# A third set of block products, its third weight block in half tiles, and stationary tiles at multiples of 128 bytes

## The chip, the cores and the metric

The kernel runs on one core of a Trainium2 chip. The metric is the time of one execution on the device in microseconds (us); smaller is better. A trace of one execution by the hardware profiler is read beside it. In the text PE is TensorE, DVE is VectorE, ACT is ScalarE, POOL is GpSimd, SP is SyncE, which issues most loads.

## The reference

The input `x` is 256 tokens by 2048. `h` is its RMS norm, and `h @ w_in` (2048 x 18,448) gives eleven groups of columns:

```
a_q a_k (1024 each)  a_v a_g (2048 each)  a_lr (16)      gated linear attention, 4 heads
b_q b_k b_v b_g (2048 each)                              differential attention, 16 heads
m_a m_b (2048 each)                                      merge gates
y_a = (rmsnorm(gla(a_q, a_k, a_v, a_lr)) * silu(a_g)) @ w_branch_a
y_b = (rmsnorm(diff(b_q, b_k, b_v)) * 0.8 * silu(b_g)) @ w_branch_b
out = x + rmsnorm((sigmoid(m_a) * y_a + sigmoid(m_b) * y_b) @ w_out)
```

All of it is float32.

## The kernel before

**A product in three.** A float32 operand is split into a high part (rounded to the type that TensorE takes at full speed, by ScalarE) and a low part (the rest, by VectorE). One product is three matmuls: high by high, low by high and high by low. `x` is split once, into `xs`. Every weight is loaded, split and used once: `emit_half` (line 215) takes a half tile of 128 x 1024 weights from the list `seq`, issues the load if it is the first half of a 1 MB tile, and has ScalarE write `hi` and VectorE write `lo`. `take` (line 239) hands a half to the matmuls and emits up to `AHEAD` = 4 halves past it. There are three `raw`, three `hi` and three `lo` buffers in `wpool`.

**Three ways to use a half.** `half_tile` (line 399), for token-major keys such as `v4`, `ag0`, `dv0`, `bg0`, `y00`, `o0`, does 12 matmuls of 512 columns with a slice of `xs` (or `oah`, `oal`, `obh`, `obl`, `mh`, `ml`) as the stationary tile and weights streaming. `half_channel` (line 420), for keys and queries, has the weights as stationary tile: 8 matmuls of 512 columns (line 427) and 8 of 256 (line 429). `block_products` (line 625) is the third.

**Sets.** A set is 1024 columns of `w_in`, done as a 2 x 2 block product with seven products in place of eight (Strassen's scheme). The operands of `x` are slices of `xs` (products 1, 2, 4) or sums of its blocks that `sum_operands` has split beforehand into eight tiles `s4h`, `s4l`, `r1h` and so on (products 3, 5, 6, 7). The order is 1, 3, 5, 6, 2, 7, 4. Each product has four steps (two tiles, two halves) of 6 matmuls of 512 columns (line 648). The weight operands are made in place, in four `chain` tiles of 1 MB: `a` starts as one block and `b` as another; after product 1 a DMA on POOL's queue that adds in flight (line 188) adds the second block to `a`; VectorE adds `b` to `a` before each step of product 6 (line 179); after product 6 the second block is added to `b` in the same way; the third block, `raw_c`, is product 2's operand, and VectorE adds it to `a` after each of that product's steps (line 186). `raw_c` is loaded as two 1 MB tiles, into two of the three `raw` slots (line 175). `link` (line 158) loads `a` and `b`. Two sets exist; their columns are the first and second half of one merge gate, and their results, `left` and `right`, become tanh values that are spilled to DRAM.

**Order of the work.** The first value groups of the linear attention come first (about 0 to 81 us). Then the mixed phase (81 to 277 us): `phase_steps` (line 70) spreads 40 other steps evenly between the 56 steps of the sets: 8 of `v4`, then 32 halves of the keys and queries of the linear attention. After it come the gates `ag0` to `ag3`, merge gates `m00` and `m01`, `diff_heads(0)` and `diff_heads(1)`, the branch product `y0`, `diff_heads(2)` and `diff_heads(3)`, the rest of the merge gates, `y1`, and `w_out`. `diff_heads(g)` (line 913) does values `dv` and gates `bg` of four heads by `token_major`, then eight query and key blocks by `channel_major`. Attention itself is cut into small tasks (generators): `pump(n)` (line 365) runs one step of the first `n` tasks in the list, between stretches of weight matmuls. `gla_scores` and `gla_out` are the linear attention's, `diff_split` and `diff_pair` the differential attention's. `y0` needs both `gla_out` tasks.

**Memory.** Pools lie one behind the other in the order in which they are opened: `const`, `wpool`, `big` (18 slots of 4 KB a partition, for `u` tiles), then `first`, which is closed after the mixed phase and followed by `small` and `more` (13 slots, for `u2` tiles). In the memory map of the compiled program `wpool` begins at byte 23,328 of a partition and `big` at 72,480, both 32 past a multiple of 128; `xs`, `mh`, `ml`, `hi` and `lo` therefore all lie 32 past one. The eight sum tiles in `first` begin at 193,888 and `more` at 165,472, both 96 past one; `oah`, `oal`, `obh`, `obl`, `ath` and `atl` lie in `more`.

Of the kernel before, what the change touches and what calls it, by code (L numbers as in the profile page):

```python
# [6 lines left out]
F32 = mybir.dt.float32  # L7
F32R = mybir.dt.float32r
# [17 lines left out]
ROWS = {"two": 2, "tok": 4, "chan": KT}  # L26
WARM = 8
PRODUCTS = (1, 3, 5, 6, 2, 7, 4)
BIG = 18
MORE = 13  # L30
BRIDGE = 512
# [3 lines left out]
def chunk_plan():  # L35

    plan = [("v0", "two", "w_in", [(6144, RANK), (2048, 2 * VG[0] - RANK)])]
    at = 2 * VG[0] - RANK
    for g, n in enumerate(VG[2:]):
        plan.append((f"v{g + 2}", "tok", "w_in", [(2048 + at, n)]))  # L40
        at += n
    for hf in range(2):
        for name, base in (("k", 1024), ("q", 0)):
            for c in range(4):
                plan.append((f"{name}{hf}{c}", "chan", "w_in", [(base + 512 * hf + P * c, P)]))
    o = 6144 + RANK
    for s in range(2):
        plan.append((f"set{s}", "set", "w_in", [(o + 10240 + 1024 * s, 1024)]))
    for g in range(4):
        plan.append((f"ag{g}", "tok", "w_in", [(4096 + 512 * g, 512)]))  # L50
        plan.append((f"dv{g}", "tok", "w_in", [(o + 4096 + 512 * g, 512)]))
        plan.append((f"bg{g}", "tok", "w_in", [(o + 6144 + 512 * g, 512)]))
        for c in range(4):
            for n, name in enumerate(("dq", "dk")):
                plan.append((f"{name}{g}{c}", "chan", "w_in", [(o + 2048 * n + 512 * g + P * c, P)]))
        plan.append((f"m0{g}", "tok", "w_in", [(o + 8192 + 512 * g, 512)]))
        for br in range(2):
            plan.append((f"y{br}{g}", "tok", ("w_branch_a", "w_branch_b")[br], [(512 * g, 512)]))
        plan.append((f"o{g}", "tok", "w_out", [(512 * g, 512)]))
    return plan  # L60
# [22 lines left out]
def hybrid_kernel(ctx: ExitStack, tc, xt, xn, preg, postg, w, w2, gkb, glag, lamv, diffg, ident_d, causal_d, lmask_d, out):  # L83
# [24 lines left out]

    def t2(shape, name):
        count[0] += 1  # L110
        return pools[0].tile(shape, F32, tag="t2", name=f"{name}_{count[0]}", bufs=6 if len(pools) == 1 else 8)

    def spill(t, name):
        count[0] += 1
# [25 lines left out]
    def halves_of(*keys):  # L140
        return [(key, r, h) for key in keys for r in range(len(at[key])) for h in range(2)]

    def heads_order(g):
        return halves_of(f"dv{g}", f"bg{g}", *(f"{name}{g}{c}" for pair in range(2) for name in ("dq", "dk") for c in (2 * pair, 2 * pair + 1)))
# [10 lines left out]
    def weights(key, r):  # L155
        a, size = at[key][r]
        return w[a : a + P * size].rearrange("(p n) -> p n", p=P), size

    def link(s, name, t):
        count[0] += 1  # L160
        c = pools[0].tile([P, 2048], F32, tag="chain", name=f"{name}_{count[0]}", bufs=4)
        sp.dma_start(c, weights(f"set{s}", {"a": 0, "b": 6}[name] + t)[0])
        chain[s, name, t] = c

    def emit_set(s, prod, t, h):
        c = slice(1024 * h, 1024 * h + 1024)
        if h == 0 and prod == 1:
            if s == 0:
                link(s, "a", t)
            link(s, "b", t)  # L170
        if h == 0 and prod == 4 and s == 0:
            link(1, "a", t)
        if h == 0 and prod == 2:
            count[0] += 1
            raws[s, t] = wpool.tile([P, 2048], F32, tag="raw", name=f"raw_c_{count[0]}")
            sp.dma_start(raws[s, t], weights(f"set{s}", 4 + t)[0])
# [3 lines left out]
        return (raws[s, t] if prod == 2 else b if prod in (3, 7) else a)[:, c]  # L180

    def follow_set(s, prod, t, h):
        c = slice(1024 * h, 1024 * h + 1024)
        a, b = chain[s, "a", t], chain[s, "b", t]
        if prod == 2:
            dve.tensor_tensor(out=a[:, c], in0=a[:, c], in1=raws[s, t][:, c], op=ALU.add)
        if h == 1 and prod in (1, 6):
            pool.dma_start(a if prod == 1 else b, weights(f"set{s}", 2 + t)[0], accum_op=ALU.add)

# [344 lines left out]
    def sum_operands():  # L534
# [5 lines left out]
        temps = []  # L540
        for n in range(2):
            count[0] += 1
            temps.append(pools[0].tile([P, 2, 8, P], F32, tag="chain", name=f"temp_{count[0]}", bufs=4))
        r1, s2, r3, s4 = (temps[n // 2][:, n % 2] for n in range(4))

        def part(i, j, q):
# [42 lines left out]
        pump()  # L589


    gspill = [None] * 4
    ts = {}

    def others():
# [29 lines left out]
    def block_products(s):  # L625
# [2 lines left out]
        left, right = u([P, 2, 512], "gl"), u([P, 2, 512], "gr")  # L628
        kept = {}

        def squash(dst, scale):
            act.activation(dst, dst, AF.Tanh, scale=scale)

        for prod in PRODUCTS:
            if prod not in bank:
# [2 lines left out]
            for t in range(2):  # L638
                for h in range(2):
# [10 lines left out]
                    if t and h:  # L650
                        if prod in (1, 5):
                            kept[prod] = t2([P, 512], f"p{prod}")
                            act.activation(kept[prod], out, AF.Copy)
                        if prod == 5:
                            kept[3] = t2([P, 512], "p35")
                            dve.tensor_tensor(out=kept[3], in0=bank[3], in1=kept[5], op=ALU.add)
                        if prod == 6:
                            dve.tensor_tensor(out=right[:, 0, :], in0=x, in1=kept[3], op=ALU.add)
                            squash(right[:, 0, :], minus_half[:, 0:1])
                        if prod == 2:  # L660
                            dve.tensor_tensor(out=left[:, 0, :], in0=out, in1=kept[1], op=ALU.add)
                            squash(left[:, 0, :], half_rstd[:, 0:1])
                        if prod == 7:
                            dve.tensor_tensor(out=right[:, 1, :], in0=x, in1=kept[5], op=ALU.add)
                            squash(right[:, 1, :], minus_half[:, 1:2])
                            gspill[2 * s + 1] = spill(right, "gr")
                        if prod == 4:
                            act.activation(left[:, 1, :], x, AF.Tanh, scale=half_rstd[:, 1:2])
                            gspill[2 * s] = spill(left, "gl")
                    yield  # L670

    sets = (step for s in range(2) for step in block_products(s))
    rest = others()
    for step in phase_steps():
        next(sets if step[0] == "set" else rest)
    for gen in (sets, rest):
        assert next(gen, DONE) is DONE
    joint.close()
    pools[0] = ctx.enter_context(tc.tile_pool(name="small", bufs=2))
    pools.append(ctx.enter_context(tc.tile_pool(name="more", bufs=MORE)))  # L680
    tasks.append(forget_gate())


# [227 lines left out]
        yield  # L911

    def diff_heads(g):
        banks = token_major(f"dv{g}", 512, x_ops, 2)
        late_u = u2 if g > 1 else u
        vv = late_u([P, 2, 512], "dv")
        for b in range(2):
            act.activation(vv[:, b, :], banks[b], AF.Copy, scale=rstd[:, b : b + 1])
        banks = token_major(f"bg{g}", 512, x_ops, 2)
        uu = late_u([P, 2, 512], "ub")  # L920
        for b in range(2):
            gate(banks[b], b, uu[:, b, :])
# [66 lines left out]
    def settle():  # L989
        while tasks:  # L990
            pump()
        gb.extend(fetch(d, "gateb", u) for d in gspill)

    mh = [u([P, 4, S], "mh", F32R) for _ in range(4)]
    ml = [u([P, 4, S], "ml", F32R) for _ in range(4)]
# [150 lines left out]
```

## Time and profile before

| | us |
|---|---|
| median of 3 runs (lowest, highest) | 1149.97 (1147.6, 1150.31) |
| the profiled execution's own time | 1149.55 |
| its span, first to last instruction | 1147.7 |
| PE busy | 1127.6 |
| DVE busy | 761.0 |
| ACT busy | 640.9 |
| POOL busy | 71.6 |

The mean granted TensorE clock of the core is 0.994 of full speed. The busy time of PE has the overlap of neighbouring matmuls in it, so it says that PE rarely stands still, and not how far it is from its best. Lines such as L407 are lines of the kernel before.

### The profile page before, as it was taken

To read this page: it belongs to the slowest core of one execution; us is meant where nothing else is said; L and a number is where in the kernel's file an instruction comes from. 1 tells how busy PE (TensorE), PEld (TensorE's weight loads), DVE (VectorE), ACT (ScalarE), POOL (GpSimd) and SP (SyncE) were. 2 spreads that over 40 slices of the span, in tenths; PEclk is the share of its full clock that TensorE was granted. 3 is DMA by queue.
4 is the path that set the end of the run, shared out by engine and by line. 5 is a ranking of instruction groups with operands and counts; after the bars stand their busy time and mean duration, and the time that the engine had idled before them with its cause. 6 is when DMAs were issued, how large, how long until landed. Compare 5 with 4: busy or idle time off the path is not lost.

```text
span 1147.7 us, 14888 instructions
## 1 busy us (share of the span) xinstructions
PE 1127.6 (98%) x5642; PEld 961.2 (84%) x5642; DVE 761.0 (66%) x1088; ACT 640.9 (56%) x957; POOL 71.6 (6%) x101
## 2 busy tenths in 40 slices
PE   9999999999999999999999999999999999999996
PEld 7999788788888888888888888888888888888886
DVE  7878876777579974577567555447666765565462
ACT  7856565556756554575656444446665665444460
POOL 0110000102031010100000000000000100000000
PEclk9999999989999999999999999999999999999998
DMA  8798777755555566355455544555455565555751
GB/s 312 263 358 226 225 294 215 193 184 184 183 190 178 200 238 257 118 177 182 148 202 186 197 164 172 182 197 176 175 173 182 191 226 177 174 179 209 275 196 74
DMA packets 37783, 230.48 MB, mean 201 GB/s; under 512 B 4752, under 2 KB 6288, under 8 KB 14672
## 3 DMA queue, kind: packets, MB, share of 16 engines
q1 hardware_dynamic: 31392, 204.89, 50.6%
q0 software_dynamic: 5312, 23.33, 7.5%
q10 hardware_dynamic: 1008, 1.32, 0.3%
q8 instruction: 44, 0.72, 0.3%
q14 instruction: 27, 0.22, 0.1%
HBM read 220.08 MB, written 9.44 MB: 200 GB/s over the span
## 4 chain that ended last, share of the span: by engine, by line
PE 93%; DMA 3%; ACT 1%; DVE 1%; issue 1%; DVEq 0%; SPq 0%; POOLq 0%; POOL 0%; ACTq 0%
PE mm L407 55%; PE mm L427 10%; PE mm L648 5%; PE mm L429 5%; PE bg L427 4%; PE bg L429 2%; DMA raw_c<-in_w_dram 2%; PE bg L390 2%; PE mm L375 2%; PE mm L390 2%; PE bg L407 1%; PE bg L748 1%; DMA raw<-in_w_dram 1%; PE bg L375 1%; PE bg L859 1%
## 5 line engine op out<-in xcount | busy, mean ns | idle before, releaser
L232 DVE TENSOR_TENSOR lo<-raw,hi 128x1024 fp32r<-128x1024 f32 (+3 forms) x355 | 428.6, 1209 | 271.8 <-ACT hi L231 268.9
L231 ACT ACTIVATE hi<-raw 128x1024 fp32r<-128x1024 f32 (+3 forms) x355 | 367.2, 1036 | 354.3 <-PE mm L407 234.6
L407 PE MATMUL mm<-hi,xs 128*128 128x512 f32 (+1 forms) x1152 | 283.4, 388 | 0.0
L407 PEld LDWEIGHTS mm<-hi,xs 128*128 128x128 f32 x1152 | 213.2, 188 | 37.8
L407 PE MATMUL mm<-lo,xs 128*128 128x512 f32 (+1 forms) x576 | 151.6, 385 | 0.0
L427 PE MATMUL mm<-xs,hi 128*128 128x512 f32 x512 | 132.8, 394 | 0.0
L407 PEld LDWEIGHTS mm<-lo,xs 128*128 128x128 f32 x576 | 108.0, 188 | 20.4
L427 PEld LDWEIGHTS mm<-xs,hi 128*128 128x128 f32 x512 | 92.3, 189 | 16.1
L429 PEld LDWEIGHTS mm<-xs,lo 128*128 128x128 f32 x512 | 69.8, 190 | 5.1
L429 PE MATMUL mm<-xs,lo 128*128 128x256 f32 x512 | 71.3, 282 | 0.0
L427 PE MATMUL bg<-xs,hi 128*128 128x512 f32 x256 | 66.9, 392 | 1.2 <-ACT hi L231 1.2
L427 PEld LDWEIGHTS bg<-xs,hi 128*128 128x128 f32 x256 | 48.1, 189 | 11.8 <-ACT hi L231 2.0
L407 PE MATMUL mm<-hi,obh 128*128 128x512 f32 x128 | 51.3, 401 | 0.0
L407 PE MATMUL mm<-hi,oah 128*128 128x512 f32 x128 | 51.1, 399 | 0.0
L870 ACT ACTIVATE prob<-prob,mx,score_scale 128x128 f32<-128x128 f32 x64 | 34.3, 537 | 29.2 <-DVE mx L865 29.2
L407 PE MATMUL mm<-hi,oal 128*128 128x512 f32 x128 | 50.6, 395 | 0.0
L407 PE MATMUL mm<-hi,obl 128*128 128x512 f32 x128 | 50.4, 394 | 0.0
L231 ACT ACTIVATE hi<-a 128x1024 fp32r<-128x1024 f32 x32 | 33.6, 1059 | 28.7 <-PE bg L427 14.7
L232 DVE TENSOR_TENSOR lo<-a,hi 128x1024 fp32r<-128x1024 f32 x32 | 38.7, 1223 | 15.9 <-ACT hi L231 14.5
L429 PEld LDWEIGHTS bg<-xs,lo 128*128 128x128 f32 x256 | 35.5, 194 | 9.7 <-DVE lo L232 7.4
L429 PE MATMUL bg<-xs,lo 128*128 128x256 f32 x256 | 36.7, 287 | 6.5 <-DVE lo L232 6.5
L321 POOL TENSOR_TENSOR de<-de,neg_half 128x2 f32<-128x2 f32 x16 | 11.5, 722 | 460.0 <-DVE de L898 460.0
(279 smaller groups left out, 1565.2 us busy)
## 6 DMA issues: line engine op xcount, KB each, us to landing
raw<-in_w_dram SPq DMA_DIRECT2D x160, 1024.0 KB, 5.0
raw<-in_w_dram SPq DMA_DIRECT2D x14, 832.0 KB, 6.4
a<-in_w_dram SPq DMA_DIRECT2D x4, 1024.0 KB, 7.5
b<-in_w_dram SPq DMA_DIRECT2D x4, 1024.0 KB, 7.5
a<-in_w_dram POOLq DMA_DIRECT2D x4, 1024.0 KB, 11.1
b<-in_w_dram POOLq DMA_DIRECT2D x4, 1024.0 KB, 8.6
raw_c<-in_w_dram SPq DMA_DIRECT2D x4, 1024.0 KB, 8.6
raw<-in_w_dram SPq DMA_DIRECT2D x4, 800.0 KB, 8.1
```

The costliest lines, as they stand in the source:

```text
L231: act.activation(hi_t[:, a:b], r[:, a:b], AF.Copy)
L232: dve.tensor_tensor(out=lo_t[:, a:b], in0=r[:, a:b], in1=f32(hi_t[:, a:b]), op=ALU.subtract)
L321: pool.tensor_tensor(out=dst, in0=src, in1=neg_half[:, : src.free_size()], op=ALU.pow)
L375: i = pe.matmul(out, lhs, rhs, start=first and n == 0, stop=last and n == len(pairs) - 1)
L390: i = pe.matmul(banks[g][b][:, :n], a[part][:, P * b : P * b + P], w[:, n * g : n * g + n], start=first, stop=last)
L407: i = pe.matmul(banks[b][:, :n], a[part][:, P * b : P * b + P], w[:, n * j : n * j + n], start=first, stop=last)
L427: i = pe.matmul(o, hi[:, c], x_pair(kt), start=kt == 0, stop=kt == KT - 1)
L429: i = pe.matmul(o[:, :S], lo[:, c], x_ops(kt)[0], start=False, stop=False)
L648: i = pe.matmul(out, a[part], w[:, 512 * j : 512 * j + 512], start=first, stop=last, skip_group_check=out is x)
L748: pe.matmul(o, xk[:, P * c : P * c + P], xq.rearrange("p (b c t) -> p b c t", b=2, c=4)[:, :, c, :], start=i == 0, stop=i == 1)
L859: pe.matmul(banks[m][:, lo:up], q2[:, m, i2, t], kh[:, m, i2, :n], start=True, stop=False)
L870: act.activation(prob[m][:, lo:up], prob[m][:, lo:up], AF.Exp, scale=score_scale[:, b : b + 1], bias=mx[:, i : i + 1], accum_out=z[:, i : ...
```

## The change

It makes three edits.

- A third set. `SETS = 3`: the 512 value columns and the 512 gate columns of the first four attention heads, which were `dv0` and `bg0`, become the set `set2`. The mixed phase has 84 steps of sets and the same 40 others. `left` of this set is the values, scaled; `right` is the gates, t times (tanh − 1) in place of a tanh alone. Both are spilled, and `diff_heads(0)` fetches them.
- The third weight block is loaded by halves of 512 KB, for all sets, into four `u` tiles of `big` instead of two `raw` slots.
- Addresses. A new pool `blocks`, opened ahead of `first`, holds the `chain` tiles and the eight sum tiles; `more` is opened ahead of `small`; `lr` (1,024 bytes a partition) moves from `big` to `const`, and a tile `margin` of 96 bytes that nothing uses is added to `const`. `const` so grows by 1,120 bytes, `wpool` begins at 24,448, and all tiles of `wpool`, `big`, `blocks` and `more` begin at multiples of 128 bytes. To make room, `first` has 5 `t2` slots instead of 6.

```diff
+SETS = 3
...
+    for s in range(2, SETS):
+        plan.append((f"set{s}", "set", "w_in", [(o + base + 512 * (s - 2), 512) for base in (4096, 6144)]))
...
-        plan.append((f"dv{g}", "tok", "w_in", [(o + 4096 + 512 * g, 512)]))
-        plan.append((f"bg{g}", "tok", "w_in", [(o + 6144 + 512 * g, 512)]))
+        if g + 2 >= SETS:
+            plan.append((f"dv{g}", "tok", "w_in", [(o + 4096 + 512 * g, 512)]))
+            plan.append((f"bg{g}", "tok", "w_in", [(o + 6144 + 512 * g, 512)]))
...
-    steps = [("set", s, prod, t, h) for s in range(2) for prod in PRODUCTS for t in range(2) for h in range(2)]
+    steps = [("set", s, prod, t, h) for s in range(SETS) for prod in PRODUCTS for t in range(2) for h in range(2)]
...
+    blocks = joint.enter_context(tc.tile_pool(name="blocks", bufs=2))
     pools = [joint.enter_context(tc.tile_pool(name="first", bufs=2))]
...
-        c = pools[0].tile([P, 2048], F32, tag="chain", name=f"{name}_{count[0]}", bufs=4)
+        c = blocks.tile([P, 2048], F32, tag="chain", name=f"{name}_{count[0]}", bufs=4)
...
-        if h == 0 and prod == 4 and s == 0:
-            link(1, "a", t)
-        if h == 0 and prod == 2:
-            count[0] += 1
-            raws[s, t] = wpool.tile([P, 2048], F32, tag="raw", name=f"raw_c_{count[0]}")
-            sp.dma_start(raws[s, t], weights(f"set{s}", 4 + t)[0])
+        if h == 0 and prod == 4 and s + 1 < SETS:
+            link(s + 1, "a", t)
+        if prod == 2:
+            raws[s, t, h] = u([P, 1024], "c")
+            sp.dma_start(raws[s, t, h], weights(f"set{s}", 4 + t)[0][:, c])
...
+    const.tile([P, 24], F32, name="margin")
...
-    lr = u([P, 2, P], "lr")
+    lr = const.tile([P, 2, P], F32, name="lr")
...
-            hi, lo = (sm([P, 8, P], f"{name}{e}", F32R, bufs=1) for e in "hl")
+            hi, lo = (blocks.tile([P, 8, P], F32R, tag=f"{name}{e}", name=f"{name}{e}", bufs=1) for e in "hl")
...
+        def right_done(b):
+            dst = right[:, b, :]
+            if s < 2:
+                act.activation(dst, dst, AF.Tanh, scale=minus_half[:, b : b + 1])
+            else:
+                t = t2([P, 512], "tanh")
+                act.activation(t, dst, AF.Tanh, scale=half_rstd[:, b : b + 1])
+                dve.scalar_tensor_tensor(out=dst, in0=t, scalar=-1.0, in1=dst, op0=ALU.add, op1=ALU.mult)
...
-    pools[0] = ctx.enter_context(tc.tile_pool(name="small", bufs=2))
-    pools.append(ctx.enter_context(tc.tile_pool(name="more", bufs=MORE)))
+    more = ctx.enter_context(tc.tile_pool(name="more", bufs=MORE))
+    pools[:] = ctx.enter_context(tc.tile_pool(name="small", bufs=2)), more
...
     def diff_heads(g):
+        if g + 2 < SETS:
+            vv, uu = (fetch(gspill[2 * g + 4 + i], name, u) for i, name in enumerate(("dv", "ub")))
+        else:
```

More of the change, by code (lines that the diff above doesn't have):

```diff
@@ L110, in t2 @@
         count[0] += 1
-        return pools[0].tile(shape, F32, tag="t2", name=f"{name}_{count[0]}", bufs=6 if len(pools) == 1 else 8)
+        return pools[0].tile(shape, F32, tag="t2", name=f"{name}_{count[0]}", bufs=5 if len(pools) == 1 else 8)
     def spill(t, name):
@@ L143, in heads_order @@
     def heads_order(g):
-        return halves_of(f"dv{g}", f"bg{g}", *(f"{name}{g}{c}" for pair in range(2) for name in ("dq", "dk") for c in (2 * pair, 2 * pair + 1)))
+        values = (f"dv{g}", f"bg{g}") if g + 2 >= SETS else ()
+        return halves_of(*values, *(f"{name}{g}{c}" for pair in range(2) for name in ("dq", "dk") for c in (2 * pair, 2 * pair + 1)))
     seq = halves_of("v0", "v2", "v3") + phase_steps()
@@ L179, in emit_set @@
             dve.tensor_tensor(out=a[:, c], in0=a[:, c], in1=b[:, c], op=ALU.add)
-        return (raws[s, t] if prod == 2 else b if prod in (3, 7) else a)[:, c]
+        return raws[s, t, h] if prod == 2 else (b if prod in (3, 7) else a)[:, c]
     def follow_set(s, prod, t, h):
@@ L185, in follow_set @@
         if prod == 2:
-            dve.tensor_tensor(out=a[:, c], in0=a[:, c], in1=raws[s, t][:, c], op=ALU.add)
+            dve.tensor_tensor(out=a[:, c], in0=a[:, c], in1=raws[s, t, h], op=ALU.add)
         if h == 1 and prod in (1, 6):
@@ L542, in sum_operands @@
             count[0] += 1
-            temps.append(pools[0].tile([P, 2, 8, P], F32, tag="chain", name=f"temp_{count[0]}", bufs=4))
+            temps.append(blocks.tile([P, 2, 8, P], F32, tag="chain", name=f"temp_{count[0]}", bufs=4))
         r1, s2, r3, s4 = (temps[n // 2][:, n % 2] for n in range(4))
@@ L589, in hybrid_kernel @@
         pump()
-    gspill = [None] * 4
+    gspill = [None] * (2 * SETS)
     ts = {}
@@ L629, in block_products, with left_done @@
         kept = {}
-        def squash(dst, scale):
-            act.activation(dst, dst, AF.Tanh, scale=scale)
+        def right_done(b):
[6 more added lines that the diff above has]
+                dve.scalar_tensor_tensor(out=dst, in0=t, scalar=-1.0, in1=dst, op0=ALU.add, op1=ALU.mult)
+        def left_done(b, src):
+            if s < 2:
+                act.activation(left[:, b, :], src, AF.Tanh, scale=half_rstd[:, b : b + 1])
+            else:
+                act.activation(left[:, b, :], src, AF.Copy, scale=rstd[:, b : b + 1])
         for prod in PRODUCTS:
@@ L658, in block_products @@
                             dve.tensor_tensor(out=right[:, 0, :], in0=x, in1=kept[3], op=ALU.add)
-                            squash(right[:, 0, :], minus_half[:, 0:1])
+                            right_done(0)
                         if prod == 2:
                             dve.tensor_tensor(out=left[:, 0, :], in0=out, in1=kept[1], op=ALU.add)
-                            squash(left[:, 0, :], half_rstd[:, 0:1])
+                            left_done(0, left[:, 0, :])
                         if prod == 7:
                             dve.tensor_tensor(out=right[:, 1, :], in0=x, in1=kept[5], op=ALU.add)
-                            squash(right[:, 1, :], minus_half[:, 1:2])
+                            right_done(1)
                             gspill[2 * s + 1] = spill(right, "gr")
                         if prod == 4:
-                            act.activation(left[:, 1, :], x, AF.Tanh, scale=half_rstd[:, 1:2])
+                            left_done(1, x)
                             gspill[2 * s] = spill(left, "gl")
                     yield
-    sets = (step for s in range(2) for step in block_products(s))
+    sets = (step for s in range(SETS) for step in block_products(s))
     rest = others()
@@ L913, in diff_heads @@
     def diff_heads(g):
[L914 to L922, printed above, removed]
+        if g + 2 < SETS:
+            vv, uu = (fetch(gspill[2 * g + 4 + i], name, u) for i, name in enumerate(("dv", "ub")))
+        else:
+            banks = token_major(f"dv{g}", 512, x_ops, 2)
+            late_u = u2 if g > 1 else u
+            vv = late_u([P, 2, 512], "dv")
+            for b in range(2):
+                act.activation(vv[:, b, :], banks[b], AF.Copy, scale=rstd[:, b : b + 1])
+            banks = token_major(f"bg{g}", 512, x_ops, 2)
+            uu = late_u([P, 2, 512], "ub")
+            for b in range(2):
+                gate(banks[b], b, uu[:, b, :])
         obh.append(u2([P, 4, S], "obh", F32R))
@@ L991, in settle @@
             pump()
-        gb.extend(fetch(d, "gateb", u) for d in gspill)
+        gb.extend(fetch(d, "gateb", u) for d in gspill[:4])
     mh = [u([P, 4, S], "mh", F32R) for _ in range(4)]
```

## The prediction

> **What bounds the kernel now.** I read the page first: which engine is busy, and what the chain that ended last is made of.
>
> ```profile
> PE 1127.6 (98%) x5642; PEld 961.2 (84%) x5642; DVE 761.0 (66%) x1088; ACT 640.9 (56%) x957; POOL 71.6 (6%) x101
> ...
> PE 93%; DMA 3%; ACT 1%; DVE 1%; issue 1%; DVEq 0%; SPq 0%; POOLq 0%; POOL 0%; ACTq 0%
> ```
>
> The chain is matmuls almost throughout, so a change counts by how many matmuls it takes away, by the time from one to the next (the pitch), and by the places where PE waits. A matmul's busy time overlaps its neighbour's; the pitch is read from the chain in order of time (start, length, line, count).
>
> ```profile
> 238.57 2.74 PE mm L648 x12
> ...
> 252.41 2.80 PE mm L648 x12
> ...
> 411.76 5.46 PE mm L407 x24
> ...
> 651.71 5.60 PE mm L407 x24
> ...
> 1053.76 61.72 PE mm L407 x272
> ```
>
> All are 512 columns wide. At 411.76 the stationary tile is `xs`, at 1053.76 `mh` or `ml`, both 32 bytes past a multiple of 128: 5.46/24 = 227.5 ns and 61.72/272 = 226.9 ns. At 651.71 it is `oah` or `oal`, 96 past: 5.60/24 = 233.3 ns. Inside the sets it is the same: 238.57 is product 2 with `xs`, 2.74/12 = 228.3 ns; 252.41 is product 7 with `r3h` and `r3l`, 96 past: 233.3 ns. No stationary tile of this kernel lies at 0 or 64, so the trace shows two addresses of four.
>
> Next the waits. PE has them in the mixed phase only (timeline of PE; the bracket is the idle time before the row), and the chain and the queue of SP say why.
>
> ```profile
> 130.66 1.21 PE L429 MATMUL bg<-xs,lo 128*128 128x256 f32 x8 [2.19 <-DVE lo L232]
> ...
> 139.38 2.12 PE L427 MATMUL bg<-xs,hi 128*128 128x512 f32 x8 [0.61 <-ACT hi L231]
> ...
> 231.12 2.07 PE L429 MATMUL bg<-xs,lo 128*128 128x256 f32 x8 [4.33 <-DVE lo L232]
> ```
>
> ```profile
> 119.35 8.80 DMA raw_c<-in_w_dram
> ...
> 233.19 2.56 PE mm L648 x6
> ```
>
> ```profile
> 71.25 32.89 SPq L203 DMA_DIRECT2D raw<-in_w_dram  x5
> 111.86 7.82 SPq L176 DMA_DIRECT2D raw_c<-in_w_dram  x2
> 133.24 9.98 SPq L203 DMA_DIRECT2D raw<-in_w_dram  x4
> ```
>
> The third weight block (`raw_c`, 1 MB a tile) takes two of the three `raw` slots. Its second tile is issued only when a key's split frees one (119.35), VectorE stands in order before the add that needs it, and the next key's load waits behind it on SP until 133.24. After the long wait PE also runs six matmuls in 2.56 us, 426.7 ns each, at half clock:
>
> ```profile
> 233.20:235.50 2.30, 2.30 (x6) 1.77 (x6) 2.30 (x4) 0.57 (x1) 0.00 (x0) 0.50 0.37 57
> ```
>
> (the 0.50 is the granted clock). Waits and slow matmuls: 2.19 + 0.61 + 4.33 + (2.56 − 6 × 0.228 = 1.19) = 8.3 us.
>
> **The change part by part.** The sum is made against the profiled execution's own 1149.55 us (span 1147.7, 1.85 around it). The median of the runs is 1149.97, 0.4 above; I correct nothing for that.
>
> *Products.* `dv0` and `bg0` leave the token-major loop: 2 keys × 8 halves × 12 = 192 matmuls at the 411.76 row, 8 × 5.46 = 43.7 us. The third set brings 7 products × 4 steps × 6 = 168, 14 times the 238.57 row, 38.4 us. Both lie on PE's chain: −5.3 us.
>
> *Addresses.* `const` grows by 1,024 + 96 bytes, so every pool behind it moves from 32 to 0; the sums go to `blocks` and `more` comes ahead of `small`, so these move from 96 to 0. Stationary tiles at 96 are in groups of these two forms (groups by line and shape, count after the x): six with `oah`, `oal`, `obh` or `obl`, 768 matmuls, and twelve with the sums, 192:
>
> ```profile
> L407 PE MATMUL mm<-hi,oah 128*128 128x512 f32 x128 | 51.1, 399 | 0.0
> ...
> L648 PE MATMUL mm<-hi,r3l 128*128 128x512 f32 x16 | 6.4, 398 | 0.0
> ```
>
> What a tile at 0 costs is not in the trace. Bounds: 213.3 ns from below (the half-clock row's 426.7 halved: the columns alone), 233.3 from above, the slowest steady pitch. I take the 226.9 of offset 32, the nearest row, and the one whose moving and stationary tiles stand in the same place to each other, as they will again. Then 768 × (233.3 − 226.9) = 4.9, 192 × (233.3 − 228.3) = 1.0, and 0.2 for 36 small ones: −6.1 us, on the chain. The Trainium skill speaks against this part: "TensorE: Matmul & The Clock Gate", Part 2, on LDWEIGHTS, says that loading the next tile's weights steals no read bandwidth from the running matmul, by which a stationary address could cost nothing and the sum would be 1140. The trace disagrees: 233.3 against 226.9 ns with the same kind of moving tile.
>
> *Third block by halves.* The block comes as four 512 KB tiles from `big`; the keys keep three `raw` slots. Of 18 slots `xs` holds 8, the set's outputs 2, keys and queries at most 4: four are left, enough for four halves, and the load can go out without waiting for a split. Nearest row for the landing (DMA issues by line, KB each, median us last):
>
> ```profile
> raw_c<-in_w_dram SPq DMA_DIRECT2D x4, 1024.0 KB, 8.6
> ```
>
> A half is written five steps ahead, about 5 × 1.9 us, so even 8.6 us is covered; uncovered, a set waits as now, 8.3/2 = 4.2 us. With that wait gone VectorE is next. The rows are the whole phase in the table of stretches (length, then busy time and count of PE, weight loads, VectorE, ScalarE, POOL), three rows of VectorE's timeline, a group, and two of the chain.
>
> ```profile
> 81.25:276.62 195.37, 187.68 (x945) 160.79 (x945) 146.99 (x150) 114.46 (x132) 14.73 (x22) 0.98 0.70 213
> ```
>
> ```profile
> 129.39 1.22 DVE L232 TENSOR_TENSOR lo<-raw,hi 128x1024 fp32r<-128x1024 f32 x1
> 130.52 1.22 DVE L232 TENSOR_TENSOR lo<-raw_c,hi 128x1024 fp32r<-128x1024 f32 x1
> 131.66 0.42 DVE L614 TENSOR_TENSOR k<-bg,k 128x256 f32<-128x256 f32 x1
> ```
>
> ```profile
> L664 DVE TENSOR_TENSOR gr<-mm,p 128x512 f32<-128x512 f32 x2 | 1.4, 680 | 0.0
> ```
>
> ```profile
> 241.31 1.81 PE bg L427 x8
> 243.12 0.95 PE bg L429 x8
> ```
>
> Over the phase it is busy 146.99 of 195.37 us (75%). The third set adds 36 × 1.22 + 6 × 0.68 = 48 us (28 splits, 8 adds, 4 sums, 2 gate products) to a phase that grows to about 230: 85%. In products 6 and 2, eight steps on end have an add beside the split: 16 × 1.13 (the distance of two such rows) = 18.1, the 3.8 key steps between them 3.8 × 1.45 = 5.5 (a split and, on average, three quarters of a 0.42 step), three sums 2.0: 25.6 us. PE needs 8 × 1.37 + 3.8 × 2.77 = 21.5 there. Today 5.7 key steps lie between, and it is 28.4 against 26.8. The shortfall rises from 1.6 to 4.1 us a set; three `hi` and three `lo` buffers cover some two steps, 3.6 us. With that cover 0.5 us a set shows, without it 3 × 4.1 = 12 us. I take half of the 8.3 as regained: −4.2 us, with ends of −8.3 and +8.3.
>
> *Moved along with it.* The third set's four accumulating loads go on POOL's queue. Their window shrinks (issue on POOL, first use on ScalarE, an interleaved `v4` step on the chain, landing times of these loads):
>
> ```profile
> 88.17 0.89 POOL L188 DMA_DIRECT2D a<-in_w_dram  x1 [4.03 <-DVE lo L232]
> 106.21 1.06 ACT L231 ACTIVATE hi<-a 128x1024 fp32r<-128x1024 f32 x1 [1.06 <-PE bg L407]
> 92.55 2.18 PE bg L407 x12
> DMA to landing us min/median/max: 8.0/9.9/12.0
> ```
>
> 18.0 us from issue to use now; 1.7 fewer interleaved steps of 2.18 leave 14.3, over the longest landing, 12.0: nothing, until a landing passes 14.3. The set's two spills and two fetches join POOL's queue ahead of the linear-attention work; values and gates of group 0 are needed only by the first attention pair, tens of us later. With `dv0` and `bg0` go 16 task steps: counted through the task list, `gla_out(1)` ends under `bg1` instead of under `dk0`, with eight key blocks (some 44 us) still ahead of `y00`, which needs it. There the fetched tiles, two attention pairs and the refetched `v` can ask for more than 18 slots; a fetch that waits on POOL holds the small powers behind it, not PE. Five `t2` slots for six touch the sums of squares at the start, which feed the norm and not the matmuls. All of this at nothing; what it could cost is inside the +8.3 above.
>
> Sum: 1149.55 − 5.3 − 6.1 − 4.2 = **1134.0 us**.
>
> **Rivals.**
> - *Zero is better than 32, not equal.* From 96 to 32 the pitch falls by 6.4 ns; a tile at 0 may fall again. About 4,240 matmuls are 400 or more columns wide (the 5,642 of the page, less 768 of L429 and 610 other narrow ones in the groups by shape, less the 24 that go): one more step is 4,240 × 6.4 = 27, 1107 us; down to the 213.3 floor, 13.6 × 4,240 = 58, 1076 us. For it: the 13.6 ns vanish at half clock, which suggests fetch and not the array, and an address can matter to fetch. Against: no row at 0. The Trainium skill, "TensorE: Matmul & The Clock Gate", section "Back-to-back issue gap", gives N/2.4 + 2.5 ns for a full clock, 215.7 at 512 columns; an estimate from it is 1134 − 4,240 × 0.0112 = 1087. No row of this trace at full clock is that low as a steady pitch.
> - *The address is not the cause.* The tiles at 96 share more than an address: they are written late, in other pools. If they stay at 233.3 the change does not do what it says: 1140 us. Against: sums and `oah` have nothing else in common, and `xs` and `mh` agree.
> - *The phase keeps or doubles its waits*, through VectorE or late loads: 1138 to 1146 us.
> - *Slower: zero is as bad as 96.* One mechanism, the pitch of every wide matmul: the some 3,244 that would be near 227 go to 233.3, +20.8; the 996 at 96 gain nothing; 1149.55 − 5.3 − 4.2 + 20.8 = 1161 us. It decides from 3.7 ns up (a pitch of 230.6), where 4,240 × 3.7 eats 5.3 + 6.1 + 4.2. Against: moving and stationary tiles keep their distance.
>
> **How the numbers follow.** Chances: forecast 0.48; one step better 0.17; down to the floor 0.11; address not the cause 0.09; waits kept or doubled 0.09; zero as bad as 96 0.06. A measurement of this kernel tells 0.3%, 3.4 us, from no change: 1146.1 to 1153.4 is "same". Faster 0.48 + 0.17 + 0.11 + 0.09 = 0.85; same 0.08, nearly all of the doubled waits; slower 0.07. The range: high 1147, the doubled waits; low, one and a quarter steps (4,240 × 8.0 = 34, 1100), the 768 of L429 with them (768 × 8.0 = 6), and the other half of the waits (4): 1090. Left out are the floor, 0.11, and the slower case, 0.06.
>
> **What would show it.** Right: rows of 24 matmuls with `oah` and `obh` at 5.45 instead of 5.60, rows with `xs` unchanged at 5.46; a set's `raw_c` gone from the chain; no bracket over 2 us on PE between 81 and 311; fourteen runs of twelve more on L648, eight rows of 24 fewer on L407. Wrong: `xs` rows at another length (the first or last rival, by sign); PE waiting for `lo` in products 6 and 2 of all three sets; `y00` waiting for `oah`.

## The result, and the profile after

The changed kernel takes 1132.88 us (median of 4 runs, 1131.6 to 1135.86) against 1149.83 us for the kernel before on the same chip (1147.6 to 1150.31): a ratio of 0.986, 95% interval 0.9836 to 0.9884, so 17 us faster. The prediction was 1134.0 us. The profiled execution of the kernel after took 1133.58 us itself, with a span of 1131.8.

The page of the kernel after first (busy time by engine, the chain that ended last by engine, and one row of the DMA issues: KB each, median us to landing):

```profile
PE 1117.8 (99%) x5618; PEld 957.4 (85%) x5618; DVE 784.2 (69%) x1112; ACT 653.6 (58%) x971; POOL 77.5 (7%) x109
...
PE 94%; DVE 2%; DMA 1%; issue 1%; ACT 1%; SPq 0%; DVEq 0%; POOLq 0%; POOL 0%; ACTq 0%
...
c<-in_w_dram SPq DMA_DIRECT2D x12, 512.0 KB, 9.1
```

PE still carries the chain, with 24 matmuls fewer. The chain in order of time gives the pitch, the time from one matmul to the next (start, length, line, count; L413 was L407, L666 was L648):

```profile
287.10 2.74 PE mm L666 x12
...
332.16 54.43 PE mm L413 x240
...
655.48 10.91 PE mm L413 x48
...
1038.09 61.68 PE mm L413 x272
```

The first row is product 7 with `r3h` and `r3l`, 2.74/12 = 228.3 ns where it was 233.3; at 655.48 the stationary tile is `oah` or `oal`, 227.3 ns where it was 233.3. `xs` at 332.16 (226.8) and `mh` at 1038.09 (226.8) stand as before.

The stages, from the start of the first matmul of each in both traces, show where the 15.9 us of span went. The start lies between 80.1 and 82.5 us in the fourteen traces of this case, so the +1.0 in its row is not put down to the change.

| us | before | after | difference |
|---|---|---|---|
| start | 81.1 | 82.1 | +1.0 |
| mixed phase (84 steps of sets for 56) | 195.1 | 226.7 | +31.5 |
| `ag`, `m00`, `m01` (before: and `dv0`, `bg0`) | 196.1 | 141.6 | −54.5 |
| `diff_heads(0)`, `(1)` without `dv0`, `bg0` | 149.9 | 158.1 | +8.2 |
| `y0` | 94.9 | 92.7 | −2.2 |
| `diff_heads(2)`, `(3)`, `m02`, `m03` | 238.2 | 240.7 | +2.5 |
| `y1` | 93.4 | 91.3 | −2.1 |
| output | 98.9 | 98.6 | −0.3 |

The third row loses 43.7 us of matmuls and 10.8 us of attention tasks, which stand in the two `diff_heads` rows instead (8.2 + 2.5). The matmul counts of these stretches agree: 258 fewer, which are the 192 of `dv0` and `bg0` and 66 of tasks, and 51 and 19 more in the two other rows. The phase gains 38.4 us of matmuls and is longer by only 31.5: some 7 us are gone there, waits and slow matmuls above all (the new places of the sums had been priced at 1.0 of it). The stretch of the whole phase (length, then busy time and count of PE, weight loads, DVE, ACT, POOL; last but two, the granted clock):

```profile
82.08:308.76 226.68, 224.39 (x1112) 191.14 (x1111) 191.34 (x192) 146.28 (x166) 19.07 (x28) 0.99 0.77 234
```

In the first two sets PE no longer waits for more than 0.3 us at a time. One longer wait stays, in the third set. Three answers carry it, the timelines of SP, of DVE and of PE (the bracket is the idle time before the row):

```profile
233.49 35.66 SPq L208 DMA_DIRECT2D raw<-in_w_dram  x4
269.19 0.96 SPq L181 DMA_DIRECT2D c<-in_w_dram  x2
```

```profile
277.87 1.23 DVE L191 TENSOR_TENSOR a<-a,c 128x1024 f32<-128x1024 f32 x1 [2.56 <-DMA c<-in_w_dram]
```

```profile
279.06 1.20 PE L666 MATMUL mm<-hi,xs 128*128 128x512 f32 x4 [1.54 <-ACT hi L236]
```

Two halves of the third block stood on SP behind four loads of the keys, each of which waits for its own slot (40.9 us in all), and went out only at 269.19. VectorE waited 2.56 us for them and PE 1.54, and from 280.4 to 283.5 the matmuls ran at a granted clock of 0.51.

### The profile page after: what moved, and what is told of

It is laid out like the page before. It is cut to its first block, busy times and chain, and to the rows that moved or that the text cites. A ratio compares the mean times of both kernels' runs of the same rounds, so it can differ in the third digit from the quotient of the medians.

```text
span 1131.8 us, 14913 instructions
## 1 busy us (share of the span) xinstructions
PE 1117.8 (99%) x5618; PEld 957.4 (85%) x5618; DVE 784.2 (69%) x1112; ACT 653.6 (58%) x971; POOL 77.5 (7%) x109
## 4 chain that ended last, share of the span: by engine, by line
PE 94%; DVE 2%; DMA 1%; issue 1%; ACT 1%; SPq 0%; DVEq 0%; POOLq 0%; POOL 0%; ACTq 0%
PE mm L413 51%; PE mm L433 10%; PE mm L666 9%; PE mm L435 5%; PE bg L433 4%; PE bg L435 2%; PE bg L396 2%; PE mm L381 2%; PE mm L396 2%; PE bg L413 2%; PE bg L766 1%; DMA c<-in_w_dram 1%; DVE lo L237 1%; PE bg L381 1%; PE bg L877 1%
## 5 line engine op out<-in xcount | busy, mean ns | idle before, releaser
L237 DVE TENSOR_TENSOR lo<-raw,hi 128x1024 fp32r<-128x1024 f32 (+3 forms) x339 | 409.4, 1209 | 250.6 <-ACT hi L236 245.1
L236 ACT ACTIVATE hi<-raw 128x1024 fp32r<-128x1024 f32 (+3 forms) x339 | 350.3, 1035 | 346.4 <-PE mm L413 217.5
L413 PE MATMUL mm<-hi,xs 128*128 128x512 f32 (+1 forms) x1024 | 251.4, 387 | 0.0
L413 PEld LDWEIGHTS mm<-hi,xs 128*128 128x128 f32 x1024 | 189.5, 188 | 33.1
L413 PE MATMUL mm<-lo,xs 128*128 128x512 f32 (+1 forms) x512 | 134.6, 385 | 0.0
L413 PEld LDWEIGHTS mm<-lo,xs 128*128 128x128 f32 x512 | 96.1, 188 | 17.9
L237 DVE TENSOR_TENSOR lo<-a,hi 128x1024 fp32r<-128x1024 f32 x48 | 58.5, 1222 | 8.8 <-ACT hi L236 8.2
L236 ACT ACTIVATE hi<-a 128x1024 fp32r<-128x1024 f32 x48 | 50.7, 1059 | 20.6 <-PE mm L666 12.3
L413 PE MATMUL mm<-hi,obh 128*128 128x512 f32 x128 | 50.7, 396 | 0.0
L413 PE MATMUL mm<-hi,oah 128*128 128x512 f32 x128 | 50.6, 395 | 0.0
L413 PE MATMUL mm<-hi,oal 128*128 128x512 f32 x128 | 49.9, 390 | 0.0
L413 PE MATMUL mm<-hi,obl 128*128 128x512 f32 x128 | 49.9, 390 | 0.0
L666 PE MATMUL mm<-hi,xs 128*128 128x512 f32 x144 | 40.2, 401 | 2.0 <-ACT hi L236 1.8
L413 PE MATMUL mm<-hi,mh 128*128 128x512 f32 x96 | 37.4, 390 | 0.0
L413 PE MATMUL mm<-hi,ml 128*128 128x512 f32 x96 | 37.4, 389 | 0.0
## 6 DMA issues: line engine op xcount, KB each, us to landing
b<-in_w_dram POOLq DMA_DIRECT2D x6, 1024.0 KB, 10.8
```

The source lines that it names most:

```text
L236: act.activation(hi_t[:, a:b], r[:, a:b], AF.Copy)
L237: dve.tensor_tensor(out=lo_t[:, a:b], in0=r[:, a:b], in1=f32(hi_t[:, a:b]), op=ALU.subtract)
L413: i = pe.matmul(banks[b][:, :n], a[part][:, P * b : P * b + P], w[:, n * j : n * j + n], start=first, stop=last)
L666: i = pe.matmul(out, a[part], w[:, 512 * j : 512 * j + 512], start=first, stop=last, skip_group_check=out is x)
```

## The experiments

Three questions: is it the place of the stationary tile that costs 6 ns; which of the three edits took the waits of the phase away; and what is the wait that is left? Times are medians; the kernel before stood at 1149.4 to 1150.1 us beside them.

**Addresses alone.** Kernel before with only the pools moved (part of the diff; the `chain` and sum tiles go to `blocks` as in the change):

```diff
+    blocks = joint.enter_context(tc.tile_pool(name="blocks", bufs=2))
...
+    const.tile([P, 24], F32, name="margin")
...
+    more = ctx.enter_context(tc.tile_pool(name="more", bufs=MORE))
+    pools[:] = ctx.enter_context(tc.tile_pool(name="small", bufs=2)), more
```

> The kernel before with nothing but the new places of the tiles (every stationary and moving tile on a multiple of 128 bytes); two sets and the third block by full tiles as before. Address theory: the rows with oah, obh and the sums fall from 233.3 to about 227 ns a matmul, rows with xs stay at 227.5, and the time is 1149.8 - 6.1 = 1143.7 us (1142 to 1145.5). Rival, the address is not the cause: those rows stay at 233 ns and the time stays at 1149 to 1151 us. Rival, the whole gain of the change is addresses and the rest worth nothing: about 1133 us.

1144.02 us, ratio 0.9951 (0.9939 to 0.9963): 5.7 us. `y0` and `y1` shorten by 2.1 us each, as in the kernel after. The size that was predicted (6.1) holds, though the 1.0 us of the sums in it is not to be seen: the phase takes 195.7 us in this trace, and 195.1 in the kernel before. What the edit changed, though, is two things: where a stationary tile lies, and how far it lies from the weights that stream past it.

**The same distance at other places.** Two kernels shift everything together, by taking the spare tile out or making it smaller:

```diff
-    const.tile([P, 24], F32, name="margin")
+    const.tile([P, 16], F32, name="margin")
```

> The kernel after without its 96 spare bytes, so that every tile of weights, sums and arrays that stood at 0 stands at 32. Theory, 32 and 0 cost the same: 227 to 228 ns everywhere and the time of the kernel after, 1132 to 1134 us. Rival, zero is a little better than 32 (0.5 to 1 ns a matmul): 4,240 x 0.5 to 1 ns, 2 to 4 us longer, 1135 to 1137 us.

> The kernel after with 64 spare bytes in place of 96, so that everything that stood at 0 stands at 96, moving and stationary tiles still at the same place to each other. Theory, the place of the stationary tile itself is what counts: 233 ns on every wide row, those with xs too; some 4,200 wide matmuls x 6.2 ns = 26 us longer, 1158 to 1160 us. Rival, only the distance of the moving from the stationary tile counts: 227 ns and 1133 us.

1131.88 us (ratio 0.9847, 0.9832 to 0.9862) and 1132.18 us (0.9848, 0.9833 to 0.9862): as the kernel after. The chain of the kernel with everything at 96, with `xs` and then `oah` as the stationary tile:

```profile
331.19 54.43 PE mm L413 x240
...
654.50 10.91 PE mm L413 x48
```

227 ns, with every one of these stationary tiles 96 past a multiple of 128. The theory that the place of the stationary tile by itself counts falls.

**Other distances.** Two kernels put the weights' buffers 64 or 96 past a multiple of 128 and all else at one (for 96: a `margin` of 16 and a `gap` of 8):

```diff
-    const.tile([P, 24], F32, name="margin")
+    const.tile([P, 8], F32, name="margin")
...
+    ctx.enter_context(tc.tile_pool(name="gap", bufs=1)).tile([P, 16], F32, name="gap")
```

> The kernel after with the buffers of the weights (raw, hi and lo) at 64 and all else at 0, so that the moving and the stationary tile of nearly every wide matmul stand 64 bytes apart modulo 128, as hi and oah did before, though no stationary tile of the wide rows with xs, oah, obh or mh stands at 96. Theory, the distance of the two counts: 233 ns on all of these rows, some 4,200 x 6.2 ns = 26 us more, 1157 to 1160 us. Rival, 96 itself is the slow place: 227 ns and 1132 to 1134 us.

> The kernel after with the weights' buffers at 96 and all else at 0: rows that stream weights against xs, oah, obh or mh have the moving tile 96 past the stationary one, rows that stream xs against weights 32 past. With 64 apart the former went to 233.3 ns and the time to 1146.0 us. Theory, only 64 apart is slow: 227 ns and 1131 to 1134 us. Rival, any distance that is not a multiple of 128 is slow: 233 ns, 1144 to 1147 us. A pitch between the two (about 230 ns) would be 1138 to 1140 us.

1145.97 us (0.9971, 0.996 to 0.9982) and 1148.33 us (0.9992, 0.9983 to 1.0002), the second 1.3 us above the range of the rival whose pitch came true. The chain, with weights at 64 and then at 96 (`xs`, then `oah` or `oal`):

```profile
332.13 55.99 PE mm L414 x240
...
659.93 11.21 PE mm L414 x48
```

```profile
336.55 55.99 PE mm L414 x240
...
665.00 11.20 PE mm L414 x48
```

233 ns in all four, with stationary tiles at multiples of 128. So the distance decides where weights stream: 0 modulo 128 gives 227 ns, 64 and 96 give 233. The same two runs hold a control: the last 108 matmuls of `w_out` stream a tile `keep`, which did not move with the weights' buffers, past the same `mh` and `ml`. They take 18.41 and 18.39 us, against 18.35 in the kernel after, while the 272 ahead of them take 63.46 in both, against 61.68.

The 26 us that I expected at 64 were 13, because my count took in rows that do not change. From the starts of single matmuls, the two large groups of 416-wide ones at the start stay at 188 to 191 ns in all these kernels, and those 256 wide behind the phase with `lo` stationary even fall from 119 to 117. The 512-wide ones with `hi` stationary behind the phase stand at 230 to 231 at a distance of 0 and of 64 and go to 233 at 32 (`xs` at 0 streaming past weights at 96), though in the phase the same form goes from 227 to 233 at both. Why these differ is open.

**The third set alone.** Kernel before with three sets, full tiles of the third block and the old addresses (part of the diff):

```diff
+SETS = 3
...
-    steps = [("set", s, prod, t, h) for s in range(2) for prod in PRODUCTS for t in range(2) for h in range(2)]
+    steps = [("set", s, prod, t, h) for s in range(SETS) for prod in PRODUCTS for t in range(2) for h in range(2)]
```

> The kernel before with the third set of products alone; third block by full tiles in the buffers of the keys, tiles where they stood. Theory: 24 matmuls fewer, -5.3 us, and a third set that waits as the two do, +4 to +5 us: 1148.5 to 1150.5 us, with waits of 2 us and more for lo in three places; oah rows at 233 ns. Rival, the set is worth more than its matmuls because the tasks moved behind it run better: under 1145 us. Rival, VectorE cannot keep up with three sets: over 1153 us.

1136.92 us, ratio 0.9891 (0.9875 to 0.9908): 12.8 us, of which the matmuls explain 5.3. Neither of my sums had this. The time lies under the 1145 us of one rival, but not for its reason, that tasks run better behind the phase: there the kernel is 44.0 us shorter than the kernel before, little more than the 43.7 of `dv0` and `bg0`. The phase is 227.27 us, almost that of the kernel after. The wait of 4.33 us in the second set is gone and the 2.19 of the first is down to 1.20 (brackets of PE's timeline), though nothing was changed about their third block.

**The halves alone.** Kernel before with the third block by half tiles, as in the diff of the change:

> The kernel before with the third weight block by half tiles alone. Theory of the prediction: the load no longer waits for a key's split, and half of the 8.3 us of waits or all of it goes: 1142 to 1146 us, no wait of PE over 2 us. Rival, the halves are worth nothing, because what they are issued behind on SP or VectorE's backlog sets the wait as well: 1148.5 to 1150.5 us.

1142.59 us, ratio 0.9936 (0.9924 to 0.9949): 7 us. With two sets the halves do what the prediction said of them, and more; two waits of PE stay, 1.73 us up to 136.52 and 1.75 up to 233.60, and ahead of each the chain has a half's landing, 6.2 and 6.3 us after an issue that stood behind a key's load.

**The kernel after without the halves** (part of the diff).

```diff
-        if prod == 2:
-            raws[s, t, h] = u([P, 1024], "c")
-            sp.dma_start(raws[s, t, h], weights(f"set{s}", 4 + t)[0][:, c])
+        if h == 0 and prod == 2:
+            count[0] += 1
+            raws[s, t] = wpool.tile([P, 2048], F32, tag="raw", name=f"raw_c_{count[0]}")
+            sp.dma_start(raws[s, t], weights(f"set{s}", 4 + t)[0])
```

> The kernel after with the third block by full tiles again, in the buffers of the keys; three sets and new addresses stay. Theory, the third set itself took the waits away (its run alone came to 1136.9, and addresses alone are worth 5.7): 1130 to 1132.5 us. Rival, the halves regain 4 us here: 1136 to 1138 us, with a wait of 4 us and more for lo.

1131.36 us, ratio 0.9839 (0.9826 to 0.9853): no slower than the kernel after, whose interval overlaps. In the change as it stands the halves are worth nothing. Addresses (5.7) and third set (12.8) alone already take the 1149.7 us of the kernel before to 1131.2 us; the 7 us of the halves are the same waits counted a second time.

**Why the third set takes waits away.** The 40 key, query and value steps are spread over 84 steps of sets in place of 56, so fewer of them fall between two steps of a set. To try that by itself, kernel before with two sets:

```diff
-        mixed += other[len(other) * i // len(steps) : len(other) * (i + 1) // len(steps)]
-    return mixed
+        mixed += other[2 * len(other) * i // (3 * len(steps)) : 2 * len(other) * (i + 1) // (3 * len(steps))]
+    return mixed + other[2 * len(other) // 3 :]
```

> The kernel before with its two sets, full tiles and addresses, but only two thirds of the key, query and value steps spread between the set's steps, as many per step as with three sets, and the rest behind the sets. No work is added or removed. Theory, the third set took waits away by spacing the keys' loads further apart, so that the third block finds its buffers free: the waits of the two sets go and the time falls by 5 to 8 us, 1142 to 1145 us. Rival, the rest of the third set's gain lies elsewhere (in what follows the phase): 1148.5 to 1151 us.

1140.94 us, ratio 0.9926 (0.9914 to 0.9939): 8.7 us from the order of the steps alone, and 1.1 us below the range that I gave. The stretch of its phase, SP's timeline in the second set, and the waits that PE has left (in this order, three views):

```profile
80.93:267.60 186.67, 184.97 (x945) 158.96 (x944) 148.07 (x150) 115.01 (x132) 19.74 (x24) 1.00 0.75 226
```

```profile
165.81 0.33 SPq L176 DMA_DIRECT2D raw_c<-in_w_dram  x1
177.56 0.33 SPq L203 DMA_DIRECT2D raw<-in_w_dram  x1
188.28 0.33 SPq L176 DMA_DIRECT2D raw_c<-in_w_dram  x1
```

```profile
126.24 2.11 PE L427 MATMUL bg<-xs,hi 128*128 128x512 f32 x8 [1.21 <-ACT hi L231]
142.06 0.50 PE L427 MATMUL bg<-xs,hi 128*128 128x512 f32 x1 [0.20 <-ACT hi L231]
```

The phase falls from 195.14 to 186.67 us with the same 945 matmuls and the same work on VectorE. The second set's two full tiles go out at 165.81 and 188.28, one key's load between them. The first lands well ahead of its use; for the second ScalarE waits 0.97 us, and PE not at all. In the kernel before SP's row for the two is `210.49 7.15 SPq L176 DMA_DIRECT2D raw_c<-in_w_dram  x2`, so the second went out at about 217, and PE's long wait began at about 227. VectorE's waits for the third block are gone: 10.5 us in three in the kernel before, none here. It is not that the tiles now find a free buffer: SP waits for a split ahead of all four of them, 40.8 us in all, where it was 31.1. They go out early enough for their use all the same, and land within 8.3 us, where it was up to 11.3; which of the two counts for more is open. So the third set's extra gain is mostly spacing. This run leaves the order behind the sets changed as well, but every later stage has the length it had before, within 0.1 us.

**Still thinner.** The same idea once more, on the kernel after with full tiles: 5/6 of the other steps spread, the rest behind the sets.

> The kernel after with full tiles of the third block (1131.4 us) and the key, query and value steps another sixth thinner between the set's steps, that sixth behind the sets. No work is added or removed. Theory, the steps between the set's products still set what is left of the waits (1.7 us at 124, 1.2 us and slow matmuls at 277): 1129 to 1130.5 us. Rival, what is left has another cause: 1131 to 1132 us.

1132.34 us, ratio 0.9854 (0.984 to 0.9869): a miss. The waits move rather than go: 1.29 us before 122.17, behind a full tile that lands only at 120.95, and 0.5 to 0.7 us in three more places.

**The wait that was left.** The kernel after with the halves given out four steps earlier:

```diff
-        if prod == 2:
+        if prod == 6:
             raws[s, t, h] = u([P, 1024], "c")
```

> The kernel after with the loads of the third block's halves given out four steps earlier, with the steps of product 6. Theory, the wait left in the third set (start gap 1.82 us and slow matmuls behind it, about 3 us above the pitch in all) is the late landing of the half behind a key's load on SP: it goes, 1129 to 1130.5 us. Rival, VectorE is behind by then anyway: 1132 to 1133.5 us with the wait in the same place, VectorE ahead of it in the chain.

1127.95 us, ratio 0.9814 (0.9799 to 0.9829): 4.9 us better than the kernel after, the intervals apart, 3.4 better than with full tiles (1131.36), and the best of all. It is even below the 1129 to 1130.5 us that I expected. The stretch of its phase, and SP's timeline in the third set:

```profile
80.77:303.17 222.40, 221.94 (x1112) 190.51 (x1112) 191.02 (x192) 146.59 (x166) 19.07 (x28) 1.00 0.78 237
```

```profile
223.17 2.63 SPq L181 DMA_DIRECT2D c<-in_w_dram  x3
231.83 0.33 SPq L208 DMA_DIRECT2D raw<-in_w_dram  x1
232.21 0.49 SPq L181 DMA_DIRECT2D c<-in_w_dram  x1
242.86 66.11 SPq L208 DMA_DIRECT2D raw<-in_w_dram  x8
```

All four halves are out by 232.70; in the kernel after the last two left at 269.19 to 270.15. VectorE has the same 191 us of work in a phase 4.3 us shorter, and PE has no wait over 0.3 us left, so VectorE was not the bound: the load was late.

**Is it the halves or the earlier issue?** The kernel after without the halves, its full tiles issued as early:

```diff
-        if h == 0 and prod == 2:
+        if h == 0 and prod == 6:
```

> The kernel after with full tiles of the third block in the buffers of the keys, given out four steps earlier, as in the run with the halves at product 6 (1127.95 us). Theory, the halves are what makes the early load possible: a full tile held some eight steps longer takes two of the three buffers of the keys and brings waits back, over 1133 us (with full tiles at product 2: 1131.4). Rival, only the earlier issue counts, whatever the tile: 1127.5 to 1129 us.

1143.94 us, ratio 0.9941 (0.9925 to 0.9956). It needs both. The trace is of the longest of six executions, 1147.04 us. There PE waits 3.57 us before 118.07 and again over 3 us in each of the other sets, and its phase is 241.89 us. The chain shows what for, here in the second set:

```profile
192.53 10.03 DMA raw<-in_w_dram
...
203.78 3.78 PE bg L434 x8
```

It is not the third block but the load of a key or value. Two of the three buffers hold full tiles that are used only later, so this load goes out when a split frees a buffer and lands 8.1 to 10.0 us after that; the matmuls behind the wait run at a granted clock of 0.50. The halves differ from the full tiles in two things, their size and buffers of their own. What PE waits for here points to the buffers; no run tells the two apart.

## Why the prediction was right, and where it was right for a wrong reason

*Products, −5.3 us.* Held: 54.5 us leave the stage of `dv0` and `bg0`, 10.8 of them tasks that stand elsewhere now, which leaves the 43.7. In the run with the third set alone 44.0 us are gone behind the phase. That 16 moved task steps cost nothing held too: 10.8 us out, 10.7 us in.

*Addresses, −6.1 us.* The size was right, 5.7 measured. The step that failed is the one that read the cost as that of "a stationary tile at 96". Of the two things that set those rows apart, I priced the place and named the distance only as a reason to expect 227 ns, and as an argument against the last rival. The runs show the distance to be the cause: everything at 96 runs at 227 ns, and weights at 64 past tiles at 0 at 233.3. Both rivals on zero (better than 32, or as bad as 96) fell; 0, 32 and 96 agree when moving and stationary tile stand alike. "The address is not the cause" fell too, since two tiles' addresses together are. The Trainium skill states in "TensorE: Matmul & The Clock Gate", Part 2, on LDWEIGHTS, that loading the next tile's weights steals no read bandwidth from the running matmul. The traces do not fit with that where the tiles are 32, 64 or 96 bytes apart and the 512-wide matmuls of the chain take 6 ns longer; whether it is the weight load that takes them, no run here tells. The Trainium skill's formula of N/2.4 + 2.5 ns (the same page, section "Back-to-back issue gap"), which that section calls the gap of an isolated matmul, gives about 216 ns at 512 columns; no row here reached it, and the lowest steady one is 226.8.

*Third block by halves, −4.2 us.* The gain was there, about 6 us (17.0 less 5.3 and 5.7), but not from this edit. The failed step is "the load can go out without waiting for a split": true of the half itself, but SP issues it in order behind loads of the keys that do wait, and in the third set it left only when they had, at 269.19. What took the waits away is something that I counted and did not price: 3.8 key steps, where there were 5.7, between the eight steps of products 6 and 2. I used that only for VectorE's shortage; in the run with the spacing alone the full tiles, too, land before VectorE needs them, although each still waits for a split on SP. With the wait gone by spacing, the halves had nothing to regain. The 8.3 us of waits was itself too low. It leaves out the eight 256-wide matmuls behind the long wait, which took 2.07 us at half clock where 0.95 is usual: 1.1 us more.

*VectorE next.* It is busy 191.34 of 226.68 us, 84%, as forecast (85%). But the shortfall of 4.1 us a set that I derived from busy times never reached PE: the run with the halves issued earlier has the same VectorE work and no wait over 0.3 us. Adding up service times over a window of eight steps overstated it, perhaps because the splits of the steps on either side can run ahead; no run tested that.

*The rest.* The accumulating loads landed in up to 16.2 us, above the 14.3 that I had named as the limit, and neither PE nor ScalarE waited for one in the phase; that limit was too strict. `y0` did not wait for `oah`. Of the signs of being right, the shorter rows with `oah` and no bracket over 2 us came; loads of the third block are not gone from the chain, they are still 1% of it. The chance of 0.08 for "same" does not follow from my own numbers: waits kept or doubled were put at 1138 to 1146 us, just under the 1146.1 at which "same" begins, so nearly all of it belonged to "faster". Two errors of my terms were of opposite sign and small (0.4 too much for addresses, 1.8 too little for waits), so the closeness of the total is partly luck.

## What to carry to other kernels

Before a gain is put down to an edit, look for other edits in the same change that can remove the same wait: here a new order of steps and new buffers for a load were each worth 7 to 9 us alone, and with the new order in place the buffers added nothing. A load is as early as the queue it is issued on: a free buffer helps only if nothing that waits stands ahead of it. And when a cost goes with an address, ask whether it is the address of one operand or the distance of two; one run that shifts both together tells.

## What the runs showed of the hardware

For the split float32 tiles of this kernel, with weights streaming, a 512-column matmul follows the last after 227 to 228 ns when the start of its moving tile and of its stationary tile agree modulo 128 bytes (both at 0, 32 or 96 tried), and after 233 ns when the moving tile stands 64 or 96 past the stationary one. With weights stationary the pitch at a distance of 32 is 233 ns as well, and at 64 it is 233 in the phase and 230 behind it, where they take 227 and 231 at a distance of 0. The 416-wide ones show no such difference (188 to 191 ns).

A load of half the size did not reliably land sooner. From issue to landing, the third block's halves of 512 KB took 9.1 us in the kernel after (median of 12) where the full tiles of 1 MB took 6.8 in the same kernel without halves (median of 6); with two sets it was 7.1 us against 8.6.
